# One run for a recurrence head's small products, with the products of its chunk states ahead of it

## The chip, the cores and the metric

The kernel runs on one core of a Trainium2 chip. A core has a matrix engine (TensorE, "PE" in the profile), a vector engine (VectorE, DVE), a scalar engine (ScalarE, ACT), GpSimd (POOL), and SyncE (SP), which here issues DMA transfers. The engines run side by side, each through its own list of instructions in a fixed order, and wait for one another by semaphores. TensorE reads its operands from the on-chip memory SBUF and writes into PSUM banks, which DVE and ACT read.

The metric is the device time of one execution in microseconds. The median of three runs before the change is 448.33 us (448.19 to 448.48).

## What is computed

One layer of a decoder: a projection of 512 tokens into many column groups, a block-sparse attention branch (8 heads of 64), a gated linear recurrence (4 heads, key and value dimension 128), two gated up-projections, an output projection and a gated embedding. The change concerns the recurrence alone. Cut to that:

```python
def hgrn2_chunkwise(q, k, v, g):          # g: logarithm of the decay, per key channel
    def step(state, inp):
        qc, kc, vc, gc = inp
        cum = jnp.cumsum(gc, axis=2)
        o_inter = jnp.einsum('bhtk,bhkv->bhtv', qc * jnp.exp(cum), state)
        diff = jnp.where(causal[:, :, None], cum[:, :, :, None, :] - cum[:, :, None, :, :], LOG_DECAY_MASK)
        scores = jnp.einsum('bhtk,bhsk,bhtsk->bhts', qc, kc, jnp.exp(diff))
        o_intra = jnp.einsum('bhts,bhsv->bhtv', scores, vc)
        last = cum[:, :, -1:, :]
        state = state * jnp.exp(last[:, :, 0, :, None]) + jnp.einsum('bhsk,bhsv->bhkv', kc * jnp.exp(last - cum), vc)
        return state, o_inter + o_intra
```

Each head thus needs the scores inside a chunk (with a decay for every pair of tokens), the state that a chunk hands on, and an output made of both. The output is normalised and gated, and goes into an up-projection.

## The kernel before

**Tiling.** The 512 tokens form four chunks of 128. Large products are split in a high and a low part (three products of 128x128 weights by 512 columns for one, 24 to a block of eight slices, L296 to L302 and L426 to L431). Weights arrive by DMA, ACT and DVE split them (`w_split`, L274), two blocks ahead.

**The recurrence head.** `hgrn_gates` (L513) makes `kb` (keys), `q` (queries, with 16 further columns of 48 for neighbours) and `cum` (the running sum of log decays). `hgrn_intra` (L537) makes the scores inside a chunk from several levels, each with its decays taken against a point between query and key: `k64` and `k32` (`kq`, L544) for far tokens, `next_to` for neighbours, `k8` and `k2` (`fours`, L573) for distances in blocks of 8 and 2. Their products are small. Into the PSUM bank `lpb` go 8 of 64 columns (L639), 8 of 32 (L644) and 16 of 48 (L600, `diag`, "own"); into the bank `lpa` go 16 of 48 for `k8` and 16 for `k2` (L600 too). TensorE makes two passes for each such product, so the profile has two records for one.

These come into the score tile `sc` in several ways: ACT copies the far blocks out (L652, L655); DVE multiplies "own" by a unit mask into `s32` (L648), lays the neighbours over it (`pred_one`, L608) and then six masked copies of the two `lpa` levels (`pred`, L617); last, four ACT copies bring `s32` onto the diagonal of `sc` (L697). All steps on `s32` follow one another on the same tile.

**The chunk state.** `turned_keys` (L660) makes decayed keys, and turns them: a transpose in blocks on DVE (L668), one DMA to DRAM (L671) and four back (L673), from SP's queue, and an ACT copy into `kd` (`turned`, L688). `hgrn_out` (L700) multiplies them with the values of three chunks (`hds`, L706, three full 128x128 products, six records) and chains the three states into `st` (L710, L713), with the decays of whole chunks read out of `cum`, whose exponential stands in `cum` itself (L686). The product `hop` (L721, L723) then takes `sc`, the values, `st` and the decayed queries (L687).

**What sets the order.** TensorE's order is the program's own order. The program counts planned time in `now`: `tick` adds the time of a piece of dense work (0.681 us for three dense products) and lets side work that is due run (`run_due`, L118), `cost` adds without that. Side work is written as generators; what they yield is either planned microseconds or a condition. HP is 2.5 us, HOP 10. `beside_attention` (L508) holds a generator until attention has emitted its next step:

```python
    def beside_attention():
        seen, until = runs[0], now[0] + BESIDE
        if seen < 1000:
            yield lambda: runs[0] > seen or now[0] >= until
```

Attention (L831) has eight steps, two for each head pair, planned 19.5 and 21 us apart; a step emits its scores (L858) and, at every first step from the second pair on, the output with the values (`o`, L906). The hop products of heads 0 to 2 wait in `hops` until a head pair's second step or the next head takes them; those of head 3 come HOP behind its states. Before the first `ub` products the program drains all four recurrence heads (`drain`, L169).

DVE, ACT, POOL and SP are put in order by the compiler's planner, by readiness and program order, with `tc.high_priority` for some. `held` (L156) makes an instruction follow the newest dense product in the planner's order; no semaphore stands for it.

In this order a head has two runs of small products: 48 behind the first `beside_attention` (L639, L644, and two groups of L600), and 16 behind the second (L694 and what follows), directly before `hds`.

**Buffers.** A tag names buffers that tiles share in turn: two for `Q` (the far keys, `k8`, `k2`), eight for `YB` (`ho`, the split results of the heads, later `mh`), two PSUM banks for `g` (`lpb`, `lpa`, `hds`), two for `KT` (`kd` and the turned keys), one for `st` and one for `s32`.

Of the kernel before, what the change touches and what calls it, by code (L numbers as in the profile page):

```python
# [11 lines left out]
F32 = mybir.dt.float32  # L12
# [22 lines left out]
H0 = 8.0  # L35

HOP = 10.0

BESIDE = 30.0

# [30 lines left out]
def hybrid_layer_kernel(  # L71
# [24 lines left out]
    scratch = ctx.enter_context(tc.tile_pool(name="scratch", bufs=2, space=bass.MemoryType.DRAM))  # L96


    BUFS = {"w": 2, "wh": 3, "wl": 3, "A": 16, "X": 16, "YB": 8, "H": 12, "T": 3, "Q": 2, "HQ": 2, "KT": 2, "SG": 4, "VV": 4, "s32": 1, "st": 1, "N": 1, "ps": 8}

    def unit(tag, name, dt=F32, shape=(128, 512)):
        return sb.tile(list(shape), dt, tag=tag, bufs=BUFS[tag], name=name)

# [36 lines left out]
    def cost(us):  # L140
        now[0] += us

    def in_order(inst):

        tc.stamp_issue_order_token(inst.ins, "side")


    dense = []

# [384 lines left out]
        V.tensor_tensor(q[:, :, 0:32], by_block(a), by_block(Q), op=OP.mult)  # L534
        hg[h] = (kb, q, cum)

    def hgrn_intra(h):  # L537
        kb, q, cum = hg[h]
        far = unit("Q", f"hx{h}", shape=(128, 1280))

        def by_block(t):
            return t.rearrange("p (k r) -> p k r", k=16)

        def kq(b, x):  # L544

            n = S // (2 * b)

            def v(t, half):
                return t.rearrange("p (n two b) -> p n two b", two=2, b=b)[:, :, half, :]
            ref = v(cum, 0)[:, :, b - 1:b].to_broadcast([128, n, b])  # L550
            in_order(V.tensor_tensor(v(x, 0), ref, v(cum, 0), op=OP.subtract))
            V.tensor_tensor(v(x, 1), v(cum, 1), ref, op=OP.subtract)
            A.activation(x, x, AF.Exp)
            V.tensor_tensor(v(x, 0), v(kb, 0), v(x, 0), op=OP.mult)
            late = q[:, :, 0:32].rearrange("p (n two g) r -> p n two g r", two=2, g=b // 32)[:, :, 1]
            x1 = v(x, 1).rearrange("p n (g r) -> p n g r", g=b // 32)
            V.tensor_tensor(x1, late, x1, op=OP.mult)
            return x
# [14 lines left out]
        def fours(b):  # L573

            x = unit("Q", f"hx{h}_{b}", shape=(128, 1280))
            keys, turned = x[:, :S], x[:, S:].rearrange("p (n r) -> p n r", r=6 * b)
            n, m = S // (4 * b), S // b

            def blocks(t):
                return t.rearrange("p (m b) -> p m b", b=b)  # L580
            ends = blocks(cum)[:, :, b - 1:b]
            in_order(V.tensor_tensor(blocks(keys), ends.to_broadcast([128, m, b]), blocks(cum), op=OP.subtract))
            late = cum.rearrange("p (n f b) -> p n f b", f=4, b=b)
            lateq = q[:, :, 0:32].rearrange("p k (n r) -> p k n r", r=4 * b)
            for w, o in runs_of(b):
                V.tensor_tensor(turned[:, :, o:o + w * b].rearrange("p n (w b) -> p n w b", w=w), late[:, :, 4 - w:, :],
                                late[:, :, 0:w, b - 1:b].to_broadcast([128, n, w, b]), op=OP.subtract)
            A.activation(x, x, AF.Exp)
            V.tensor_tensor(keys, kb, keys, op=OP.mult)
            for w, o in runs_of(b):  # L590
                t_ = turned[:, :, o:o + w * b].rearrange("p (k n) r -> p k n r", k=16)
                V.tensor_tensor(t_, lateq[:, :, :, (4 - w) * b:], t_, op=OP.mult)
            return x
# [23 lines left out]
                V.copy_predicated(late(s32), late(m), src.rearrange("p c (n r) -> p c n r", r=6 * b)[:, :, :, o:o + w * b])  # L617


        k64 = kq(64, far[:, 0:S])  # L620
        yield HP
        k32 = kq(32, far[:, S:2 * S])
        yield HP
        next_to()
        yield HP
# [2 lines left out]
        yield from beside_attention()  # L628
        while hops:
            hops.pop()()  # L630
        lpb = bank("g", f"lpb{h}")
        big = lpb[:, 256:512].rearrange("p (c t) -> p c t", c=NT)
        own = lpb[:, 0:192].rearrange("p (c t) -> p c t", c=NT)
        lpa = bank("g", f"lpa{h}")[:, 0:384].rearrange("p (l c t) -> p l c t", l=2, c=NT)

        for c in range(NT):
            for half in range(2):
                o, i = c * 128 + 32 * half, 64 * (c % 2) + 32 * half
                PE.matmul(big[i:i + 32, c // 2, :], k64[:, o:o + 32], k64[:, c * 128 + 64:c * 128 + 128],  # L639
                          start=True, stop=True)  # L640
        for c in range(NT):
            for half in range(2):
                o, i = c * 128 + 64 * half, 64 * (c % 2) + 32 * half
                PE.matmul(big[i:i + 32, 2 + c // 2, 0:32], k32[:, o:o + 32], k32[:, o + 32:o + 64], start=True, stop=True)  # L644
        cost(0.3)
        diag(own, kb, q)
        diag(lpa[:, 0], k8[:, :S], by_block(k8[:, S:]))
        V.tensor_tensor(s32, own[:, :, 0:32], eye[:, None, :].to_broadcast([128, NT, 32]), op=OP.mult)  # L648
        scv = sc.rearrange("p (i two) t -> p i two t", two=2)
        for par in range(2):  # L650
            i = 64 * par
            A.activation(scv[0:64, :, par, 64:128], big[i:i + 64, 0:2, :], AF.Copy)  # L652
            for half in range(2):
                j = 64 * half
                A.activation(scv[j:j + 32, :, par, j + 32:j + 64], big[i + 32 * half:i + 32 * half + 32, 2:4, 0:32], AF.Copy)  # L655
        pred_one(own[:, :, 32:48])
        yield HP
        nk = 3 * 128

# [18 lines left out]
            kd, kts = turned_keys()  # L678
            yield HP
        k2 = fours(2)  # L680
        yield 3 * HP
        if not h:
            kd, kts = turned_keys()
        yield 4.0 if h else 8.0

        A.activation(cum, cum, AF.Exp)  # L686
        V.tensor_tensor(q[:, 4:, 0:32], q[:, 4:, 0:32], cum[:, 128:].rearrange("p (k r) -> p k r", r=32), op=OP.mult)  # L687
        turned = A.activation(kd[:, :nk].rearrange("p (c g k) -> p g c k", c=3, g=4),  # L688
                              kts[:, :nk].rearrange("p (g c k) -> p g c k", g=4, c=3), AF.Copy)
        held(turned) if h == 0 else held_from(2.0, [turned], f"hds{h}")  # L690
        yield from beside_attention()
        diag(lpa[:, 1], k2[:, :S], by_block(k2[:, S:]))
        for i in range(2):
            pred(i, lpa[:, i])  # L694
        for g in range(4):
            s_ = slice(32 * g, 32 * g + 32)
            A.activation(sc[s_, :, s_], s32[s_], AF.Copy)  # L697
        hg[h] += (kd,)

    def hgrn_out(h, vb, sbg):  # L700
        kb, q, cum, kd = hg[h][:4]
        hv = slice(h * 128, h * 128 + 128)
        dsp = bank("g", f"hds{h}")
        done.add(f"hds{h}")
        for c in range(3):
            PE.matmul(dsp[:, c * 128:c * 128 + 128], kd[:, c * 128:c * 128 + 128], vb[c][:, hv],  # L706
                      start=True, stop=True)
        cost(0.65)
        st = unit("st", f"st{h}", shape=(128, 3, 128))
        V.tensor_copy(st[:, 0], dsp[:, 0:128])  # L710
        for c in (1, 2):
            e = c * 128 + 127
            V.scalar_tensor_tensor(st[:, c], st[:, c - 1], cum[:, e:e + 1], dsp[:, c * 128:c * 128 + 128],  # L713
                                   op0=OP.mult, op1=OP.add)
        op_ = []

        def products():
            op_.append(bank("a", f"hop{h}"))
            for c in range(NT):
                s_ = slice(c * 128, c * 128 + 128)  # L720
                PE.matmul(op_[0][:, s_], vb[c][:, hv], sc[:, c, :], start=True, stop=(c == 0))  # L721
                if c:
                    PE.matmul(op_[0][:, s_], st[:, c - 1], q[:, 4 * c:4 * c + 4, 0:32], start=False, stop=True)  # L723
            cost(1.5)

        if h < GH - 1:
            hops.append(products)
            yield lambda: op_
        else:
            yield HOP  # L730
            products()
        op_ = op_[0]
        o = unit("YB", f"ho{h}")
        y = unit("N", f"hy{h}")
        A.activation(o, op_, AF.Square)
        gated = f"bg{h}" in done
        if gated:
            V.scalar_tensor_tensor(sbg[h], op_, ogain[:, h:h + 1], sbg[h], op0=OP.mult, op1=OP.mult)
        token_spread(y, token_factor(token_sums(o, y, 1.0 / 128)))
        if gated:  # L740
            V.tensor_tensor(sbg[h], sbg[h], y, op=OP.mult)
        else:
            V.scalar_tensor_tensor(o, op_, ogain[:, h:h + 1], y, op0=OP.mult, op1=OP.mult)
        hg[h] += (None if gated else o,)
# [16 lines left out]
    def recurrence(vb, sbg, res):  # L761
        for h in range(GH):
            yield lambda: h in hg
            if h == 0:
                yield H0
            yield from hgrn_intra(h)
            spawn(hgrn_rest(h, vb, sbg, res))
            yield HP

# [625 lines left out]
```

## Time and profile before

| What | Value |
|---|---|
| median of three runs | 448.33 us (448.19 to 448.48) |
| the profiled execution, its own time | 448.74 us |
| its span on the core | 447.0 us |
| ACT busy | 289.2 us (65%) |
| POOL busy | 89.3 us (20%) |
| instructions | 7843 |

The profile shows one execution. Times inside it count from the start of the span. A row of the chain in order of time has the start, the duration and the line with the number of instructions; a row of a timeline adds the tiles, their sizes and, in brackets, the idle time ahead of it and what ended it. Groups give the busy time and the mean in ns. A matmul's end is modelled, so TensorE is better read by the starts of successive products than by its busy share. The span leaves out 448.74 - 447.0 = 1.7 us around it.

### The profile page before, as it was taken

How to read it: one execution, taken by the hardware profiler on the slowest of the kernel's cores; microseconds unless marked ns; L12 is line 12 of the kernel's file. 1: busy time of each engine (PE TensorE's matmuls, PEld its weight loads, DVE VectorE, ACT ScalarE, POOL GpSimd, SP SyncE). 2: the span in 40 equal slices, each digit the busy share in tenths (PEclk: the TensorE clock that was granted, in tenths of full speed). 3: DMA queues.
4: the chain of work that ended last, by engine and by line, in shares of the span. 5: the costliest groups of instructions: out<-in, count | busy, mean ns of one | idle time of the engine just before them, and what ended most of it. 6: DMA issues, size and time to landing. Idle time of an engine off the chain costs nothing.

```text
span 447.0 us, 7843 instructions
## 1 busy us (share of the span) xinstructions
PE 442.9 (99%) x2808; PEld 374.0 (84%) x2808; DVE 338.7 (76%) x678; ACT 289.2 (65%) x549; POOL 89.3 (20%) x155
## 2 busy tenths in 40 slices
PE   9999999999999999999999999999999999999997
PEld 8888888888888888888888888878888888899996
DVE  5769496786989797958989475565479869998844
ACT  5858484646689888967988697865235434555421
POOL 1000100010000323040402141411210103425520
PEclk9999999999999999999999999999999999999999
DMA  8802333168594464273423643356641544312111
GB/s 253 336 1 95 117 119 114 52 206 189 168 233 130 137 174 134 75 197 119 128 71 109 201 130 132 87 166 167 209 154 46 170 145 154 119 48 94 49 48 47
DMA packets 31958, 59.51 MB, mean 133 GB/s; under 512 B 7088, under 2 KB 16944, under 8 KB 31920
## 3 DMA queue, kind: packets, MB, share of 16 engines
q0 software_dynamic: 10848, 34.87, 24.7%
q1 hardware_dynamic: 20928, 24.14, 19.0%
q8 instruction: 22, 0.36, 0.4%
q14 instruction: 16, 0.13, 0.1%
q10 hardware_dynamic: 144, 0.01, 0.0%
HBM read 48.78 MB, written 4.98 MB: 120 GB/s over the span
## 4 chain that ended last, share of the span: by engine, by line
PE 99%; DVE 0%; issue 0%; DVEq 0%
PE gb L300 10%; PE ga L300 10%; PE h L300 10%; PE g L1260 9%; PE bq L300 5%; PE ub L300 5%; PE aq L430 5%; PE ag L300 5%; PE ak L430 5%; PE bf L300 5%; PE bg L300 5%; PE av L430 5%; PE ua L300 5%; PE bi L430 5%; PE pe L300 2%; PE o L906 2%
## 5 line engine op out<-in xcount | busy, mean ns | idle before, releaser
L282 DVE TENSOR_TENSOR wl<-wf,wh 128x1024 fp32r<-128x1024 f32 (+1 forms) x70 | 77.9, 1112 | 34.5 <-ACT wh L281 34.1
L281 ACT ACTIVATE wh<-wf 128x1024 fp32r<-128x1024 f32 (+1 forms) x70 | 67.0, 958 | 47.6 <-PE ub L300 10.3
L271 POOL DMA_DIRECT2D wf<-in_w_tr_dram x30 | 16.1, 538 | 113.0 <-DVE wl L282 78.1
L893 POOL DMA_DIRECT2D pb<-pb x56 | 27.6, 501 | 38.9 <-DVE pb L882 17.0
L300 PE MATMUL ga<-xh,wh 128*128 128x512 f32 x64 | 25.2, 394 | 0.0
L300 PE MATMUL gb<-xh,wh 128*128 128x512 f32 x64 | 25.1, 393 | 0.0
L300 PE MATMUL ga<-xh,wl 128*128 128x512 f32 x64 | 24.9, 389 | 0.0
L300 PE MATMUL gb<-xl,wh 128*128 128x512 f32 x64 | 24.9, 389 | 0.0
L300 PE MATMUL ga<-xl,wh 128*128 128x512 f32 x64 | 24.9, 389 | 0.0
L300 PE MATMUL h<-mh,wh 128*128 128x512 f32 x64 | 24.9, 389 | 0.0
L300 PE MATMUL h<-ml,wh 128*128 128x512 f32 x64 | 24.9, 389 | 0.0
L300 PE MATMUL h<-mh,wl 128*128 128x512 f32 x64 | 24.9, 389 | 0.0
L300 PE MATMUL gb<-xh,wl 128*128 128x512 f32 x64 | 24.9, 389 | 0.0
L877 ACT ACTIVATE pb<-pb,ps 128x128 f32<-128x128 f32 (+3 forms) x32 | 17.6, 551 | 7.6 <-DVE ps L875 7.0
L271 POOL DMA_DIRECT2D wf<-in_w_tok_dram x8 | 4.4, 550 | 80.8 <-DVE wl L282 77.7
L1236 ACT ACTIVATE sg<-sg 128x256 f32<-128x256 f32 x12 | 5.0, 414 | 20.3 <-DVE sg L1233 20.3
L271 POOL DMA_DIRECT2D wf<-in_w_up_dram x16 | 8.6, 539 | 40.6 <-DVE wl L282 28.1
L879 ACT ACTIVATE pb<-pb,ps 128x128 f32<-128x128 f32 (+3 forms) x32 | 15.8, 550 | 0.1
L300 PEld LDWEIGHTS ga<-xh,wh 128*128 128x128 f32 x64 | 12.0, 188 | 2.8 <-issue 0.4
L300 PEld LDWEIGHTS gb<-xh,wh 128*128 128x128 f32 x64 | 12.0, 188 | 2.8 <-issue 0.2
L300 PEld LDWEIGHTS gb<-xh,wl 128*128 128x128 f32 x64 | 12.0, 188 | 2.5
L300 PEld LDWEIGHTS ga<-xh,wl 128*128 128x128 f32 x64 | 12.0, 188 | 2.5
(956 smaller groups left out, 1449.1 us busy)
## 6 DMA issues: line engine op xcount, KB each, us to landing
wf<-in_w_tr_dram POOLq DMA_DIRECT2D x30, 512.0 KB, 3.8
wf<-in_w_tok_dram POOLq DMA_DIRECT2D x8, 512.0 KB, 3.5
wf<-in_w_up_dram POOLq DMA_DIRECT2D x16, 256.0 KB, 3.0
wf<-in_w_o_dram POOLq DMA_DIRECT2D x8, 512.0 KB, 4.4
wf<-in_w_g_dram POOLq DMA_DIRECT2D x8, 512.0 KB, 3.7
wf<-in_w_tok_dram SPq DMA_DIRECT2D x6, 512.0 KB, 6.9
bias<-in_ed_dram SPq DMA_DIRECT2D x8, 256.0 KB, 4.9
xres<-in_xT_dram SPq DMA_DIRECT2D x8, 256.0 KB, 2.7
```

Of the source, the lines that this page charges most:

```text
L271: (G if len(wraw) >= FAR else nc.sync).dma_start(raw, ap)
L281: rounds[i] = A.activation(hi, wraw[i], AF.Copy)
L282: low = V.tensor_tensor(lo, wraw[i], hi.bitcast(F32), op=OP.subtract)
L300: dense.append(PE.matmul(ps, a[:, k, :], b[k], start=(n == 0), stop=(n == tot - 1)))
L430: dense.append(PE.matmul(banks[t], a[:, s_], b[:, kk, :], start=(k == 0 and i == 0), stop=(k == KD - 1 and i == 2)))
L877: A.activation(p_, p_, AF.Exp, bias=st[:, 0:1], scale=-1.0, accum_out=st[:, 1:2])
L879: A.activation(p_, p_, AF.Copy, scale=st[:, 2:3])
L893: (G if both and b % 2 else nc.sync).dma_start(pt[32 * b:32 * b + 32, a], z[32 * a:32 * a + 32, b])
L906: PE.matmul(o[64 * j:64 * j + 64, qs], va[kb][:, h0:h0 + 64], pt[:, :, 4 * b_ + o0 // 128 + kb, :], start=(kb == 0), stop=(kb == qb))
L1236: A.activation(t[:, c], ps, AF.Sigmoid)
L1260: dense.append(PE.matmul(dst[i], a[:, k], b, start=(m == 0 and i in (1, 6, 5)), stop=(m == 11), skip_group_check=i not in (1, 6, 5)))
```

## The change

The three `hds` products and the chain of states move out of `hgrn_out` into `hgrn_states`, which `hgrn_intra` calls 3 planned us (STATES) behind the ACT copy of the turned keys. That copy is now due 2.5 us behind `k2`'s code for heads 1 to 3, where it was 11.5, and 4 us behind the turned keys for head 0, where it was 8. The decays of whole chunks get a tile of their own, `decay` (128x3). The 48 products move behind the second `beside_attention`, in front of the 16 of `k2`, so that all 64 come in one run; the copies out of their banks move with them, and for the last head they have a higher priority in the planner. hq's scaling moves behind them. `k64` and `k32` become two `YB` tiles instead of one `Q` tile, and `YB` gets a ninth buffer. Head 0's first instruction of `k2` is held behind the newest dense product.

```diff
+STATES = 3.0
...
-    BUFS = {... "YB": 8, ...}
+    BUFS = {... "YB": 9, ...}
...
-        k64 = kq(64, far[:, 0:S])
+        k64 = kq(64, unit("YB", f"hx{h}_64"))
         yield HP
-        k32 = kq(32, far[:, S:2 * S])
+        k32 = kq(32, unit("YB", f"hx{h}_32"))
...
         yield from beside_attention()
         while hops:
             hops.pop()()
-        lpb = bank("g", f"lpb{h}")
...
-        diag(own, kb, q)
-        diag(lpa[:, 0], k8[:, :S], by_block(k8[:, S:]))
...
-        pred_one(own[:, :, 32:48])
         yield HP
...
         k2 = fours(2)
-        yield 3 * HP
+        yield HP if h else 3 * HP
         if not h:
             kd, kts = turned_keys()
-        yield 4.0 if h else 8.0
-
-        A.activation(cum, cum, AF.Exp)
-        V.tensor_tensor(q[:, 4:, 0:32], q[:, 4:, 0:32], cum[:, 128:].rearrange("p (k r) -> p k r", r=32), op=OP.mult)
+            yield 4.0
+        decay = sb.tile([128, 3], F32, tag="decay", bufs=2, name=f"hd{h}")
+        A.activation(decay, cum.rearrange("p (c t) -> p c t", c=NT)[:, 0:3, 127], AF.Exp)
         turned = A.activation(kd[:, :nk].rearrange("p (c g k) -> p g c k", c=3, g=4),
                               kts[:, :nk].rearrange("p (g c k) -> p g c k", g=4, c=3), AF.Copy)
         held(turned) if h == 0 else held_from(2.0, [turned], f"hds{h}")
+        yield STATES
+        st = hgrn_states(h, kd, decay, vb)
+        yield 2 * HP
+        A.activation(cum, cum, AF.Exp)
+        yield HP
         yield from beside_attention()
+        lpb = bank("g", f"lpb{h}")
...
+        diag(own, kb, q)
+        diag(lpa[:, 0], k8[:, :S], by_block(k8[:, S:]))
         diag(lpa[:, 1], k2[:, :S], by_block(k2[:, S:]))
...
+        with tc.high_priority(offset=AHEAD if h == GH - 1 else 0):
+            V.tensor_tensor(s32, own[:, :, 0:32], eye[:, None, :].to_broadcast([128, NT, 32]), op=OP.mult)
...
+            pred_one(own[:, :, 32:48])
+            for i in range(2):
+                pred(i, lpa[:, i])
+            V.tensor_tensor(q[:, 4:, 0:32], q[:, 4:, 0:32], cum[:, 128:].rearrange("p (k r) -> p k r", r=32), op=OP.mult)
+            for g in range(4):
+                s_ = slice(32 * g, 32 * g + 32)
+                A.activation(sc[s_, :, s_], s32[s_], AF.Copy)
+        hg[h] += (st,)
...
+    def hgrn_states(h, kd, decay, vb):
         hv = slice(h * 128, h * 128 + 128)
         dsp = bank("g", f"hds{h}")
         done.add(f"hds{h}")
...
-            V.scalar_tensor_tensor(st[:, c], st[:, c - 1], cum[:, e:e + 1], dsp[:, c * 128:c * 128 + 128],
+            V.scalar_tensor_tensor(st[:, c], st[:, c - 1], decay[:, c:c + 1], dsp[:, c * 128:c * 128 + 128],
                                    op0=OP.mult, op1=OP.add)
+        return st
```

More of the change, by code (lines that the diff above doesn't have):

```diff
@@ L96, in hybrid_layer_kernel @@
     scratch = ctx.enter_context(tc.tile_pool(name="scratch", bufs=2, space=bass.MemoryType.DRAM))
-    BUFS = {"w": 2, "wh": 3, "wl": 3, "A": 16, "X": 16, "YB": 8, "H": 12, "T": 3, "Q": 2, "HQ": 2, "KT": 2, "SG": 4, "VV": 4, "s32": 1, "st": 1, "N": 1, "ps": 8}
+    BUFS = {"w": 2, "wh": 3, "wl": 3, "A": 16, "X": 16, "YB": 9, "H": 12, "T": 3, "Q": 2, "HQ": 2, "KT": 2, "SG": 4, "VV": 4, "s32": 1, "st": 1, "N": 1, "ps": 8}
     def unit(tag, name, dt=F32, shape=(128, 512)):
@@ L145, in in_order @@
         tc.stamp_issue_order_token(inst.ins, "side")
+        return inst
     dense = []
@@ L535, in hgrn_gates, with hgrn_intra @@
         hg[h] = (kb, q, cum)
-    def hgrn_intra(h):
+    def hgrn_intra(h, vb):
         kb, q, cum = hg[h]
-        far = unit("Q", f"hx{h}", shape=(128, 1280))
         def by_block(t):
@@ L581, in fours @@
             ends = blocks(cum)[:, :, b - 1:b]
-            in_order(V.tensor_tensor(blocks(keys), ends.to_broadcast([128, m, b]), blocks(cum), op=OP.subtract))
+            first = in_order(V.tensor_tensor(blocks(keys), ends.to_broadcast([128, m, b]), blocks(cum), op=OP.subtract))
+            if b == 2 and h == 0:
+                held(first)
             late = cum.rearrange("p (n f b) -> p n f b", f=4, b=b)
@@ L630, in hgrn_intra @@
             hops.pop()()
-        lpb = bank("g", f"lpb{h}")
[L632 to L645, printed above, removed]
-        diag(own, kb, q)
-        diag(lpa[:, 0], k8[:, :S], by_block(k8[:, S:]))
[L648 to L655, printed above, removed]
-        pred_one(own[:, :, 32:48])
         yield HP
@@ L690, in hgrn_intra @@
         held(turned) if h == 0 else held_from(2.0, [turned], f"hds{h}")
-        yield from beside_attention()
-        diag(lpa[:, 1], k2[:, :S], by_block(k2[:, S:]))
[L693 to L701, printed above, removed]
+        yield STATES
+        st = hgrn_states(h, kd, decay, vb)
@@ new lines, in hgrn_intra @@
+        yield 2 * HP
+        A.activation(cum, cum, AF.Exp)
+        yield HP
+        yield from beside_attention()
+        lpb = bank("g", f"lpb{h}")
+        big = lpb[:, 256:512].rearrange("p (c t) -> p c t", c=NT)
+        own = lpb[:, 0:192].rearrange("p (c t) -> p c t", c=NT)
+        lpa = bank("g", f"lpa{h}")[:, 0:384].rearrange("p (l c t) -> p l c t", l=2, c=NT)
+        for c in range(NT):
+            for half in range(2):
+                o, i = c * 128 + 32 * half, 64 * (c % 2) + 32 * half
+                PE.matmul(big[i:i + 32, c // 2, :], k64[:, o:o + 32], k64[:, c * 128 + 64:c * 128 + 128],
+                          start=True, stop=True)
@@ new lines, in hgrn_intra @@
+        for c in range(NT):
+            for half in range(2):
+                o, i = c * 128 + 64 * half, 64 * (c % 2) + 32 * half
+                PE.matmul(big[i:i + 32, 2 + c // 2, 0:32], k32[:, o:o + 32], k32[:, o + 32:o + 64], start=True, stop=True)
+        cost(0.3)
+        diag(own, kb, q)
+        diag(lpa[:, 0], k8[:, :S], by_block(k8[:, S:]))
+        diag(lpa[:, 1], k2[:, :S], by_block(k2[:, S:]))
+        with tc.high_priority(offset=AHEAD if h == GH - 1 else 0):
+            V.tensor_tensor(s32, own[:, :, 0:32], eye[:, None, :].to_broadcast([128, NT, 32]), op=OP.mult)
+            scv = sc.rearrange("p (i two) t -> p i two t", two=2)
+            for par in range(2):
+                i = 64 * par
+                A.activation(scv[0:64, :, par, 64:128], big[i:i + 64, 0:2, :], AF.Copy)
+                for half in range(2):
+                    j = 64 * half
+                    A.activation(scv[j:j + 32, :, par, j + 32:j + 64], big[i + 32 * half:i + 32 * half + 32, 2:4, 0:32], AF.Copy)
+            pred_one(own[:, :, 32:48])
[5 more added lines that the diff above has]
+                A.activation(sc[s_, :, s_], s32[s_], AF.Copy)
@@ L711, in hgrn_out @@
         for c in (1, 2):
-            e = c * 128 + 127
-            V.scalar_tensor_tensor(st[:, c], st[:, c - 1], cum[:, e:e + 1], dsp[:, c * 128:c * 128 + 128],
+            V.scalar_tensor_tensor(st[:, c], st[:, c - 1], decay[:, c:c + 1], dsp[:, c * 128:c * 128 + 128],
                                    op0=OP.mult, op1=OP.add)
+        return st
+    def hgrn_out(h, vb, sbg):
+        kb, q, cum, st = hg[h][:4]
+        hv = slice(h * 128, h * 128 + 128)
         op_ = []
@@ L765, in recurrence @@
                 yield H0
-            yield from hgrn_intra(h)
+            yield from hgrn_intra(h, vb)
             spawn(hgrn_rest(h, vb, sbg, res))
```

## The prediction

> **What bounds the kernel.** I read the page's busy times first, then the shares of the chain that ended last, then the waits of PE alone.
>
> ```profile
> span 447.0 us, 7843 instructions
> PE 442.9 (99%) x2808; PEld 374.0 (84%) x2808; DVE 338.7 (76%) x678; ACT 289.2 (65%) x549; POOL 89.3 (20%) x155
> ...
> PE 99%; DVE 0%; issue 0%; DVEq 0%
> ```
> ```profile
> PE warm L195 <- PEq L1383: 0.8, 1, 0.8
> ```
>
> TensorE is busy for 442.9 of 447.0 us, the chain is TensorE's own work, and the one wait of PE in the whole run is 0.8 us before its first product. So nothing that DVE, ACT or a DMA does sets the end today. The change can gain only by making TensorE's own list of products shorter; it loses whatever it makes TensorE wait. No stall is there to be removed.
>
> The list itself is read in the chain in order of time (start, duration, line, count). Head 0 lies inside the aq and ak projections, with no attention near it:
>
> ```profile
> 80.12 0.36 PE lpb L639 x16
> 80.48 0.12 PE lpb L644 x16
> 80.60 0.36 PE lpb L600 x28
> 80.97 0.34 PE lpa L600 x24
> 81.31 2.26 PE aq L430 x9
> ...
> 100.57 0.48 PE lpa L600 x32
> 101.05 0.86 PE hds L706 x6
> 101.92 4.80 PE ak L430 x21
> ```
>
> Head 1 has its first run behind scores and its second behind an attention output:
>
> ```profile
> 154.82 0.36 PE lpb L639 x16
> ...
> 156.01 5.66 PE bq L300 x24
> 161.67 10.88 PE gb L300 x48
> ...
> 180.38 0.48 PE lpa L600 x32
> 180.85 0.86 PE hds L706 x6
> 181.72 1.39 PE bg L300 x6
> ```
>
> And near the end come a hop run and a scores run that go straight back to dense products:
>
> ```profile
> 288.86 0.44 PE hop L721 x4
> ...
> 290.42 6.85 PE ga L300 x30
> 297.27 0.90 PE s L858 x6
> 298.17 3.62 PE ga L300 x15
> ```
>
> The reader is to see four prices. A dense product costs 10.88 / 48 = 0.2267 us. Dense products behind a run of another shape cost more: bq 5.66 - 24 x 0.2267 = 0.22 behind the small products, ga 3.62 - 15 x 0.2267 = 0.22 behind scores, but ga only 6.85 - 30 x 0.2267 = 0.05 behind hop, whose products use the whole array like the dense ones. The second lpa group costs 0.48 where it opens a run, while an equal group that follows another costs 0.34: 0.14 to enter. And hds, six records of a 128-column product, costs 0.86 behind lpa, where hop's records of that size cost 0.44 / 4 = 0.11 each, 0.66 for six: 0.20 for the change of shape.
>
> **The products, part by part.** The change adds and drops none. In the old order a head has a run of 48 (8 + 8 + 16 + 16, two records each), and later a run of 16 followed at once by the three hds. In the new one hds goes alone, some 10 planned us earlier, and all 64 go in one run.
>
> Head 0 before: 81.31 - 80.12 = 1.19 for the first run and 2.26 - 9 x 0.2267 = 0.22 to leave it; 101.92 - 100.57 = 1.35 for the second and 4.80 - 21 x 0.2267 = 0.04 to leave it. Sum 2.80. After: hds between dense products like hop, 0.66 + 0.05; the run of 64, 0.36 + 0.12 + 0.36 + 0.34 + 0.34 = 1.52, and 0.22 to leave it. Sum 2.45, so 0.35 less.
>
> Heads 1 to 3 before, by head 1: 156.01 - 154.82 = 1.19 and 0.22; 181.72 - 180.38 = 1.34 and 1.39 - 6 x 0.2267 = 0.03. Sum 2.78. After, the scores at that place lead back to dense products themselves (0.22), hds costs 0.71, the run of 64 behind the attention output 1.52, and 0.22 to leave. Sum 2.67, so 0.11 less, times three 0.33. All four heads: **about 0.7 us less**. From below, if the longer run and the lone hds keep the full entry prices (0.14 each, eight times 0.14 = 1.1), it would be 0.4 us more; from above, if every dropped border is worth 0.22, see the third rival. I take 0.7, since each term is a row of the same products.
>
> The Trainium skill (TensorE: Matmul & The Clock Gate, section Back-to-back issue gap) gives a product of up to 64 columns a floor of about 25 ns. By it 64 products take 1.6 us in however many runs they come, an estimate, and the gain shrinks by 0.08 a head to 0.4 us. The rows above have 16 products in 0.34 us, 21 ns each, so I keep the rows.
>
> **The order around them.** TensorE's order is the program's, so I added up the due times in the code in steps of 0.681 (three dense products). Head 0's run of 64 now falls behind ak; its planned cost then counts inside the delay before the first scores, which therefore come two dense steps (1.36 us) earlier among the dense products, and the later scores with them by one or two. For heads 1 to 3, hds comes 17 steps behind the first scores of a head pair's second step; the head asks for its place beside attention 29 steps behind, and the next scores come at 31. So the run of 64 stands where the 16 and hds stood, and no head is later.
>
> Does hds wait? Its keys are turned through DRAM, and ACT copies them back before it:
>
> ```profile
> L688 ACT ACTIVATE hkd<-hkt x4: 507/509/512, 95.2 to 270.0; 128x384 f32<-128x384 f32 x4
> ...
> L673 SPq DMA_DIRECT2D hkt<-hkt2there x4: 331/426/490, 188.1 to 189.4; - x4
> ...
> DMA to landing us min/median/max: 1.7/2.0/4.5
> ```
> ```profile
> 273.55 0.65 PE s L858 x7
> ```
>
> Head 2's keys land by 189.4 + 4.5 = 194 us, and its hds, now behind 228.85 (quoted below), moves 15 dense steps and the scores and values of a step ahead, to about 214, so the DMA has 20 us. The copy is tied to a dense product only two steps (1.36 us) ahead of hds and takes 0.51. Today head 3's copy is tied to a product one step before the scores at 273.55, that is at 272.9, yet it ran at 270.0: ACT keeps about 2.9 us ahead of that tie. So I cost this wait at nothing; without that lead it would be 0.51 plus what ACT is in the middle of (under 1.1 us, a weight rounding) less 1.36, up to 0.3 us a head. Behind the copy on ACT stand gate and rounding work that TensorE needs one or two blocks later.
>
> The remaining edits lie off TensorE. The decay tile adds one tiny ACT instruction a head:
>
> ```profile
> 90.35 0.23 ACT L312 ACTIVATE qy<-qt 128x32 f32<-128x32 f32 x1
> ```
>
> At most 0.23 us each by this row, on an engine that is busy 65%: nothing. The states' three DVE instructions move from the crowded stretch behind attention's scores to an emptier one. The keys k64 and k32 in YB buffers, with a ninth, issue the same instructions, live longer, and free the Q buffers sooner; by my count nine YB buffers hold the worst moment (two of head 3, ho of head 2, six finished halves). Head 0's turned keys have the same place; those of the others are issued no later, so SP gets the same transfers. Each is covered by DVE and ACT work that TensorE does not wait for today.
>
> What does lose cover is the tail: the masked copies, the diagonal copies and hq's scaling of the whole head now start only behind the run of 64, and hop needs them all.
>
> ```profile
> 233.28 0.25 DVE L617 COPY_PREDICATED s<-mkf,lpa 128x96 f32<-128x96 int32 x1
> ...
> 243.42 0.31 DVE L617 COPY_PREDICATED s<-mkf,lpa 128x96 f32<-128x96 int32 x1
> ...
> 245.31 0.50 DVE L617 COPY_PREDICATED s<-mkf,lpa 128x64 f32<-128x64 int32 x2
> ...
> 251.51 0.75 DVE L738 SCALAR_TENSOR_TENSOR bg2s<-hop,sm,bg2s 128x512 f32<-128x512 f32 x1 [5.70 <-ACT ho L735]
> ```
> ```profile
> 245.85 1.27 ACT L697 ACTIVATE sc<-s 32x128 f32<-32x128 f32 x4 [1.09 <-DVE s L617]
> ```
> ```profile
> 228.85 0.48 PE lpa L600 x32
> ...
> 249.28 0.44 PE hop L721 x4
> ```
> ```profile
> L687 DVE TENSOR_TENSOR hq<-hq,hu 128x384 f32<-128x384 f32 x4 | 2.2, 540 | 0.0
> ...
> L608 DVE COPY_PREDICATED s<-mkf,lpb 128x64 f32<-128x64 int32 x4 | 1.2, 303 | 0.0
> ...
> L648 DVE TENSOR_TENSOR s<-lpb,mkf 128x128 f32<-128x128 f32 x4 | 1.1, 283 | 0.0
> ```
>
> Head 2's copies end at 245.85 + 1.27 = 247.12, and hop starts at 249.28: 2.16 us of slack. From run to hop it is 27 steps now instead of 28, 1.52 + 0.22 + 27 x 0.681 = 20.1 us instead of 20.4, so 1.9 us of slack remain before anything is added. Added are 0.28 + 0.30 + 0.54 = 1.1 us of DVE work and two more links in the chain, less three state instructions. DVE runs dry behind 245.31 for 5.70 us, so if the late links fall into that gap they cost about 0.3 each, and 1.2 us of slack are left. I cost it at nothing.
>
> **The rivals.** (1) **hop waits for the masked copies** at heads 1 and 2. The first and the fourth copy, with two between, put the links (243.42 - 233.28) / 3 = 3.4 us apart while DVE is full. Two more such links are 6.8 us; the point from which it decides is 1.9 us of added chain. It costs between 0 and 6.8 - 1.9 = 4.9 us at head 2, and less at head 1. For it: the links really are that far apart. Against it: the gap of 5.70 us. With 3 us of wait it gives 448.7 - 0.7 + 3 = 451.0, by the median 450.6: slower. Chance 0.22, small waits elsewhere (a rounding moved by the new DVE order) with it.
>
> (2) **The order is not what I added up**: a head misses its place, which has two steps of margin, and its run comes 27 steps later. Head 3's hop would then follow the scores at 297.27 by more than ten us and the ub products would wait: over 15 us, about 465. Chance 0.02, since the same sum gives every position of the old order.
>
> (3) **Every border between shapes costs its full 0.22.** Head 0 loses two borders (4 to 2), the others one each (7 to 6): five, 1.1 us, 447.2 by the median. For it: both exits into dense products show 0.22. Against it: hds shows 0.20, and the entry 0.14. Chance 0.18. The Trainium skill (TensorEngine Tiling (Array Packing), section Key Properties) says that a change of tiling mode drains TensorE; that is this rival's rule, and the 0.22 behind scores against 0.05 behind hop agrees with it.
>
> **How the numbers follow.** The profiled execution took 448.74, its span 447.0; the median of the runs is 448.33, 0.41 below. 448.74 - 0.7 = 448.0, by the median **447.6**. The forecast itself has 0.58. Its own range, from 0.9 less to 0.4 more, is 447.4 to 448.7; with the third rival below and the milder half of the first above, the range is 447.0 to 450.6. A measurement can tell about 0.2% (0.9 us) from no change: faster, under 447.4, has 0.21 (the third rival and an edge of the forecast); slower, over 449.2, 0.22 (most of the first rival and the second); within 0.57.
>
> **What would show it.** In the chain of the changed kernel hds should stand alone between dense products at about 0.7 us, the run of 64 at about 1.5, and no PE wait beyond the first 0.8. A PE wait at hop on the copies into sc would be the first rival; at hds on ACT's copy, the small price above; scores and run of 64 apart, the second. A smaller hds that is not near 0.7, or dense products behind it with more than 0.05, would break the sum.

## The result, and the profile after the change

The kernel after the change takes **451.73 us** (median of 6 runs, 450.80 to 451.78), the one before 448.36 (6 runs, 448.01 to 448.51): 1.0071 times as long, with a 95% interval of 1.0058 to 1.0084. The forecast was 447.6, its range 447.0 to 450.6. It was wrong in sign and the time lies above the range.

The profiled execution took 451.19 us, with a span of 449.4. First the same three views as before the change: busy times, shares of the chain, waits of PE.

```profile
span 449.4 us, 7830 instructions
...
PE 443.1 (99%) x2808; PEld 372.9 (83%) x2808; DVE 339.0 (75%) x678; ACT 289.0 (64%) x553; POOL 89.2 (20%) x155
...
q8 instruction: 22, 0.36, 0.3%
...
PE 95%; ACT 2%; DVE 1%; issue 1%; DVEq 0%; ACTq 0%
```
```profile
PE lpa L602 <- issue: 1.7, 2, 1.0
...
PE gb L302 <- DVE hk L526: 0.3, 1, 0.3
PE aq L432 <- DVE wl L284: 0.2, 1, 0.2
```

TensorE is as busy as before (443.1 for 442.9), but it now waits. Two waits follow on DVE work; the largest, 1.7 us in two pieces, has "issue" as its cause: nothing that the profile records. The chain in order of time of the kernel after shows where (start, duration, line, count), with head 0, where all is well, for comparison:

```profile
107.19 0.36 PE lpb L680 x16
...
108.04 0.68 PE lpa L602 x48
108.72 2.94 PE bg L302 x12
...
228.03 0.36 PE lpb L680 x16
...
228.88 0.64 PE lpa L602 x45
229.52 0.70 issue
230.22 0.28 PE lpa L602 x5
230.50 0.89 PE bg L302 x3
...
277.36 0.36 PE lpb L680 x16
...
278.72 0.96 issue
279.68 0.38 PE lpa L602 x15
280.05 10.47 PE ga L302 x45
```

At head 0 the run of 64 costs 108.72 - 107.19 = 1.53 and the exit 2.94 - 12 x 0.2267 = 0.22. At head 2 TensorE stops in the middle of the run, and the run costs 230.50 - 228.03 = 2.47; at head 3, 280.05 - 277.36 = 2.69. Against 1.52 that is 0.95 and 1.17, **2.1 us** in all. (The rows of the chain list only some of the small products. The groups of instructions over the same stretches have all 128 records of each run; by them TensorE stops behind the 123rd at head 2 and behind the 112th at head 3.) Head 1, not shown, costs 1.53 like head 0.

The two waits on DVE are read in a timeline, with DVE beside PE (in brackets the idle time and what ended it):

```profile
72.04 0.39 PE L432 MATMUL aq<-wh,xl 128*128 128x512 f32 x1
72.63 0.50 PE L432 MATMUL aq<-wl,xh 128*128 128x512 f32 x1 [0.20 <-DVE wl L284]
72.97 0.39 PE L432 MATMUL aq<-wh,xh 128*128 128x512 f32 x1
...
166.06 0.40 PE L302 MATMUL gb<-xh,wl 128*128 128x512 f32 x1
166.73 0.50 PE L302 MATMUL gb<-xh,wh 128*128 128x512 f32 x1 [0.28 <-DVE hk L526]
167.07 0.40 PE L302 MATMUL gb<-xl,wh 128*128 128x512 f32 x1
```
```profile
64.06 2.10 DVE L588 TENSOR_TENSOR hx<-hu 128x384 f32<-128x384 f32 x6
...
71.39 2.31 DVE L284 TENSOR_TENSOR wl<-wf,wh 128x1024 fp32r<-128x1024 f32 x2
...
166.00 0.68 DVE L526 TENSOR_TENSOR hk<-ha,bf 128x512 f32<-128x512 f32 x1
```

Successive starts say more than the bracket: a dense product follows the last by 0.2267 us, but here by 0.59 and then by 0.34, so the aq wait costs 0.59 + 0.34 - 2 x 0.2267 = 0.48 with its restart, and gb in the same way 0.67 + 0.34 - 0.45 = 0.56. A smaller wait stands ahead of bg at 135.6, where the weight load waits for ACT's softmax (pb, L888): 0.30.

The DVE rows carry the cause of the first. Before the change three subtractions stood at that place:

```profile
64.81 1.10 DVE L586 TENSOR_TENSOR hx<-hu 128x384 f32<-128x384 f32 x3
```

Now there are six, 1.0 us more. k64 and k32 no longer take a `Q` buffer, so `fours(2)` of head 0 finds one free, and only its first instruction is held. The other three subtractions slip in front of hq's product and the weight split, and TensorE waits for both.

So the sum for the kernel after is: 2.12 in the two runs, 0.48 + 0.56 + 0.30 in three waits, less 0.68 of shorter borders (the prediction's sum): 2.8 us. The medians differ by 3.4. In the two chains all heads lie between the first aq and the first ub product, and this stretch takes 301.79 - 60.40 = 241.39 us before the change and 304.13 - 59.65 = 244.48 after it, 3.09 more. (Ahead of aq the profile of before has 0.75 more, in the first products of all, which the change does not touch.)

### The profile page after: what moved, and what is told of

The parts are those of the page before. It is cut to its first block, busy times and chain, and to the rows that moved or that the text cites. A ratio compares the mean times of both kernels' runs of the same rounds, so it can differ in the third digit from the quotient of the medians.

```text
span 449.4 us, 7830 instructions
## 1 busy us (share of the span) xinstructions
PE 443.1 (99%) x2808; PEld 372.9 (83%) x2808; DVE 339.0 (75%) x678; ACT 289.0 (64%) x553; POOL 89.2 (20%) x155
## 4 chain that ended last, share of the span: by engine, by line
PE 95%; ACT 2%; DVE 1%; issue 1%; DVEq 0%; ACTq 0%
PE ga L302 10%; PE h L302 10%; PE g L1271 9%; PE gb L302 9%; PE bg L302 5%; PE ub L302 5%; PE bf L302 5%; PE ak L432 5%; PE ag L302 5%; PE ua L302 5%; PE av L432 5%; PE bi L432 5%; PE aq L432 5%; PE bq L302 4%; PE pe L302 2%; PE o L917 2%
## 5 line engine op out<-in xcount | busy, mean ns | idle before, releaser
L284 DVE TENSOR_TENSOR wl<-wf,wh 128x1024 fp32r<-128x1024 f32 (+1 forms) x70 | 76.5, 1094 | 37.1 <-ACT wh L283 34.5
L888 ACT ACTIVATE pb<-pb,ps 128x128 f32<-128x128 f32 (+3 forms) x32 | 17.6, 551 | 6.9 <-DVE ps L886 6.9
L893 DVE STREAM_TRANSPOSE pb<-pb 128x512 f32<-128x512 f32 x20 | 13.1, 689 | 2.0 <-ACT pb L890 2.0
```

What stands on the lines that cost most here:

```text
L284: low = V.tensor_tensor(lo, wraw[i], hi.bitcast(F32), op=OP.subtract)
L888: A.activation(p_, p_, AF.Exp, bias=st[:, 0:1], scale=-1.0, accum_out=st[:, 1:2])
L893: V.transpose(z[:, :, b_, :].rearrange("p b (n c) -> p b n c", c=32), pb[:, b_].rearrange("p (n b c) -> p b n c", b=4, c=32))
```

## The experiments

**Theory 1** is that the long run outruns the supply of TensorE's instructions. The page has 22 packets of instructions with 0.36 MB: 16.4 KB each. TensorE has 2808 products and 2808 weight loads; 5616 / 22 = 255, so a packet is about 256 instructions, and one small product (two loads and two products) is four of them. A run of 64 is thus one whole block, used up in 1.5 us. **Theory 2**, a rival, is that k2's tile comes late and the record of that wait is missing. **Theory 3** is that the rest of the loss are the waits on DVE and ACT from a new order of their work.

| Run | Kernel | Median us (runs) | Ratio to before, 95% |
|---|---|---|---|
| e1_shift | after, list moved by 160 | 449.88 (10) | 1.0028, 1.0018 to 1.0038 |
| e5_block | after, list moved by 256 | 451.27 (4) | 1.0072, 1.0058 to 1.0086 |
| e11_shift48 | after, list moved by 48 | 451.09 (4) | 1.0059, 1.0047 to 1.0072 |
| e6_before_shift | before, list moved by 160 | 448.16 (10) | 1.0003, 0.9994 to 1.0012 |
| e2_k2first | after, k2's products first in the run | 450.18 (1) | single run, no interval |
| e3_split | after, run cut in 48 and 16 | 451.49 (4) | 1.0070, 1.0052 to 1.0087 |
| e4_due_hold | after, scores 1.38 later, k2 held | 454.55 (4) | 1.0140, 1.0110 to 1.0171 |
| e7_shift_hold | moved by 160, k2 held | 448.87 (11) | 1.0017, 1.0009 to 1.0026 |
| e8_shift_hold_due | moved by 148, held, scores 1.38 later | 450.21 (5) | 1.0045, 1.0032 to 1.0058 |
| e10_shift_hold_step | moved by 160, held, scores 0.7 later | 447.74 (11) | 0.9990, 0.9982 to 0.9999 |
| e9_states | after, run of 48 back at its old place | 451.55 (6) | 1.0075, 1.0060 to 1.0089 |

Before took 448.50 beside e1 to e4, 448.04 beside e5 to e8 and 448.36 beside e9 to e11.

### e1_shift: the same work, another place in the list

```diff
-    for i in range(WARM):
+    for i in range(5):
         PE.matmul(warm[:, 0:128], one, one, start=True, stop=True)
+    for i in range(44):
+        j = 32 * (i % 4)
+        PE.matmul(warm[j:j + 32, 0:32], one[:, 0:32], one[:, 0:32], start=True, stop=True)
```

The first products write a bank that nobody reads; here 4 of them are left out and 44 small ones added, 160 instructions more, all ahead of the first weights.

> The changed kernel, with TensorE's list of instructions moved by 160: of its nine first products (which compute nothing that is used) five stay and 44 small ones of the same kind follow, at about the time of the four left out. Nothing else differs. Theory 1 (TensorE runs out of fetched instructions in the run of 64: 256 instructions in 1.5 us, and the two gaps of 0.70 and 0.96 us in the lpa products of heads 2 and 3 are a block of instructions that has not landed): the block borders fall elsewhere in the run, both gaps go or move to another head, and PE's wait for nothing, 1.7 us, changes by over 0.5 us. Theory 2 (the k2 factors or the bank come late): both gaps stay within 0.2 us.

1.85 us less than the kernel after, for a change that touches no head. In the chain of this kernel head 2's run has no gap:

```profile
229.03 0.36 PE lpb L683 x16
...
229.88 0.68 PE lpa L605 x64
230.56 0.90 PE bg L305 x3
```

### e5_block, e11_shift48, e6_before_shift: the controls

e5 has 68 small products in place of 44 (256 instructions, a whole block); e11 keeps 8 of the first products and adds 13 small ones (48); e6 is e1's edit on the kernel before.

> The kernel after, with TensorE's list moved by 256 instructions (4 of the 9 unused first products left out, 68 small unused ones added): one whole block of instructions. Theory 1 (a run of 64 outruns the supply where a block's border falls at its start): a block's border lies again where it lay in the kernel after, so the two gaps inside lpa at heads 2 and 3 are back, 0.5 to 1.2 us each at the same place near the run's end, and the time is 451.0 to 452.0. Rival (the shift by 160 helped because the start of the kernel is another, or because the added products warm something up): no gaps, 449.9 as with the shift by 160.

> The kernel after with its list moved by 48 instructions only (1 of the 9 unused first products left out, 13 small ones added). From the places of the gaps so far, a block's border stands 10 instructions ahead of head 2's run in the kernel after, 32 ahead of head 3's and 16 inside head 1's, and the next 256 later. Theory 1: moved by 48, the border stands 32 ahead of head 1's run, as it did at head 3, so head 1, which had no gap, gets one of 0.7 to 1.2 us about 48 records into lpa; heads 2 and 3, with borders 58 and 80 ahead, amid the slower o products, have none or under 0.2. Time: the kernel after less 2.1 plus 1.0, 450.2 to 450.9. Rival (gaps belong to the heads, to their data or their place in time): gaps again at heads 2 and 3 and none at head 1, or at none, 449.9.

> The kernel before, with its list moved by 160 as in the first experiment (4 unused first products left out, 44 small ones added). Theory 1: a run of 48 with its 192 instructions never holds a whole block beside dense products, so there is no gap with either place of the borders, and the time is that of before, 448.4 within 0.3. Rival (the shift itself gains, whatever the runs): about 1.8 us less, 446.6.

The chain of e5, heads 2 and 3, and then that of e11, head 1 and head 2:

```profile
229.84 0.64 PE lpa L605 x59
230.48 0.69 issue
...
279.16 0.51 PE lpa L605 x48
279.67 0.67 issue
280.35 0.38 PE lpa L605 x15
```
```profile
181.08 0.49 PE lpa L605 x35
181.58 0.95 issue
182.53 0.40 PE lpa L605 x17
...
230.62 0.68 PE lpa L605 x48
231.30 0.91 PE bg L305 x3
```

Moved by a whole block, both gaps are back at the same products, behind the 123rd and the 112th record. Moved by 48, the gap leaves heads 2 and 3 and appears at head 1, as worked out beforehand from the places of the borders; e11's time is 0.2 us above the expected range. The kernel before does not care for the shift (1.0003; from the first aq to the first ub product its chain takes 241.39 us with the shift, as without). So the gap belongs to the place in the list, not to a head, its data or the warming products.

The transfers fit. In a narrow window of the view of DMA, here 227.8 to 228.0 of the kernel after, one packet of instructions starts, right at the beginning of head 2's run:

```profile
DMA packets 1, 0.02 MB, mean 82 GB/s; under 512 B 0, under 2 KB 0, under 8 KB 0
...
q8 instruction: 1, 0.02, 28.7%
```

The share, 28.7% of 16 engines for 0.2 us, is 0.92 us for this packet. TensorE goes on at 230.22, 2.2 to 2.4 us after the packet's start. The same reading gives 2.5 to 2.7 at head 3 (packet between 277.0 and 277.2, resumed at 279.68), 2.3 to 2.5 and 2.2 to 2.5 in e5, 2.5 to 2.7 in e11, and 2.2 to 2.6 in the five gaps of e2 and e4 (below). A block asked for at a border can be used only some 2.5 us later, and a run of 64 eats the block before it in 1.5. By this reading the gap, about 1 us, comes when a border falls close to the start of a run; with the border further off, the block also holds slower products of o or dense ones. A packet at the start of a run is not enough: at head 1 of the kernel after one starts between 179.4 and 179.6, the run at 179.61, and there is no gap. Its border can be counted from the gaps that head 1 gets when instructions are added ahead of it: behind record 111, 222 instructions in, with 48 added (e11), and behind record 129, 258 in, with 12 (e4, below). Both put it 14 instructions inside the run of the kernel after (222 + 48 - 256 and 258 + 12 - 256), so the block ends only seven dense products, 1.6 us, behind the run. The old runs of 48 and 16 hold 192 and 64 instructions, never a whole block.

The Trainium skill (Runtime: NRT & Kernel Launch, section Instruction fetch mechanics) says that instructions are refilled in blocks of 16 KiB, 256 of them, and that the next is fetched while the present one executes; the 16.4 KB above agree. It also calls the cost of a border "mostly hidden", since dispatch is slower than the fills; by that the run would cost 1.5 everywhere, and the gaps of 0.67 to 0.96 here speak against it for products of 21 ns.

### e2_k2first and e3_split: is k2 late, and what a cut costs

e2 moves k2's 16 products from the end of the run to its front; e3 puts a planned 2.5 us between the 48 and the 16.

```diff
+        yield HP
         diag(lpa[:, 1], k2[:, :S], by_block(k2[:, S:]))
```

> The changed kernel with the 16 products of k2 at the front of the run of 64 instead of its end. Theory 1 (instructions run out): the gap stays where it is counted in instructions, near the end of the run, now in the k8 products, still 0.7 and 1.0 us at heads 2 and 3. Theory 2 (k2 comes late): the gap stands in front of the run or behind its first products, at k2.

> The changed kernel with 2.5 planned us of dense products between the 48 and the 16 products of k2. Theory 1 (instructions run out): neither part has 256 instructions, the gaps of heads 2 and 3 go (2.1 us with what they cost behind them), and each head pays another border, 0.14 + 0.22, 1.4 us in all: 0.5 to 1 us faster than the changed kernel, about 451. If the run's length had nothing to do with it, it would be 1.4 us slower than the changed kernel, about 453.

With k2 first, the gaps stand near the run's end as before, now inside k8's products, which had long been ready, and behind the 123rd and the 112th record again (chain of e2, head 2):

```profile
227.46 0.48 PE lpa L602 x32
...
228.65 0.30 PE lpa L602 x27
228.94 0.56 issue
229.50 0.28 PE lpa L602 x5
```

Theory 2 falls. Cut in two, the run has no gap, yet next to nothing is won: 451.49 is 0.24 below the kernel after, where 0.5 to 1 was expected, and the intervals overlap. Each head pays its border again, and head 3's outputs, later now, make ub wait (waits of PE in e3):

```profile
PE ub L302 <- ACT ybh L233: 0.6, 1, 0.6
```

### e4, e7, e8 and e10: the waits on DVE and ACT

e4 holds all four subtractions of head 0's k2 and moves the first scores by 1.38 planned us; e7 is e1 with the holding alone; e8 and e10 add the scores' move to it, by 1.38 and by 0.7. The edits:

```diff
-                V.tensor_tensor(turned[:, :, o:o + w * b]...
+                then = V.tensor_tensor(turned[:, :, o:o + w * b]...
...
+                if b == 2 and h == 0:
+                    held(then)
...
-        yield 5.0 - BIAS0
+        yield 5.0 - BIAS0 + 0.7
```

> The changed kernel with attention due 1.38 planned us later, so that its steps stand where they stood before among the dense products, and with all four subtractions of head 0's k2 held behind the newest dense product instead of the first alone. Theory 3 (the rest of the loss, about 1.2 us, is TensorE waiting for a split weight in aq, because k2's subtractions stand in front of it on DVE, and for PSUM banks in gb and bg, because scores come two dense steps earlier): these three waits go, 0.9 to 1.3 us faster than the changed kernel, and the gaps in the run of 64 stay or move a little, as the list differs by some 12 instructions at heads 1 to 3. Otherwise: within 0.3 us of the changed kernel.

> The first experiment (list moved by 160) and all four subtractions of head 0's k2 held behind the dense product, where the kernel after holds only the first. Theory 3 (three subtractions of 0.35 us ahead of hq's product and of the weight split on DVE make the aq products wait): the two aq waits (0.9 on hq, 0.2 on the split, about 1.3 to 1.5 lost with their restart) go, and 449.9 falls to 448.3 to 448.7, the time of before. Rival (DVE has slack there, the waits are of one profile only): 449.9 stays.

> As the run before it, and the first scores due 1.38 planned us later, so that they stand among the dense products where they stood before the change; the list is moved by 148, since this order puts 12 more instructions ahead of the runs of heads 1 to 3. Theory 3: the waits of gb on hk (0.3 to 0.6) and of bg on pb (0.2 to 0.4) go too, no gap in the instruction supply is left, and the time is 447.5 to 448.1, below before. Rival (moving the scores brings the wait of o on the masked softmax, 1.3 us with 0.4 of small gaps around it, as it did with the unmoved list): 449.0 to 449.8.

> The list moved by 160, the four subtractions of head 0's k2 held, and the first scores due 0.7 planned us later: each head pair's first scores then come one dense step earlier than before the change (two in the kernel after), its second scores and o where they stood before (one step earlier in the kernel after, one later with 1.38). Theory 3: o does not wait (it did where the scores stood a step too late), the wait of gb on hk (0.56 in the place lost) gets smaller or goes, and the time lies between 447.5 and 448.4, at or below before. Rival (waits come back elsewhere at any place of the scores): 448.9 or more, as without the move.

e4 was a miss. The waits of aq, gb and bg went, but the order put 12 more instructions ahead of the runs of heads 1 to 3. The gaps of heads 2 and 3 moved by just that: they stand behind the 117th and the 106th record, six records and their six weight loads earlier. At head 1 a border now fell just behind the run, and the scores, a dense step too late at head 2, made o wait (waits of PE in e4):

```profile
PE bg L302 <- issue: 1.8, 1, 1.8
PE lpa L604 <- issue: 1.5, 2, 0.8
PE o L919 <- DVE ps L888: 1.3, 1, 1.3
```

These 4.6 us outweigh what was won. In e8, moved by 148 to undo the 12, no gap was left, but the wait of o stayed: 450.21, a little above its rival's range. Of e7 the profile has neither aq wait; against e1 the ratio falls by 0.0011, 0.5 us, where 1.3 to 1.5 was expected, and the two intervals overlap. The 0.9 us wait on hq in e1's profile, taken from the slowest of its ten runs (450.22), is probably too large for the typical one (the kernel after has 0.2, on the weight load alone). What remains in e7 is gb's 0.3 and, on the weight load, the wait of bg on the softmax. In e10 the view of waits of PE has one row only, the wait ahead of its first product that all these kernels have:

```profile
PE warm L197 <- PEq L1399: 0.8, 1, 0.8
```

447.74 us, 0.62 below before, interval 0.9982 to 0.9999. This version has the whole change in it, with the list moved, k2 held and the first scores 0.7 later, and it beats both kernels, narrowly.

### e9_states: half of the change

> Half of the change: the chunk states' products stand ahead as in the kernel after, but the run of 48 is back at its old place, so each head has a run of 48, hds alone and a run of 16; the rest (decay tile, YB buffers for k64 and k32, the one held subtraction) is as after. By the prices read in the chain, head by head: 1.19 + 0.22 and 0.67 + 0.05 and 0.48 + 0.22, 2.83 instead of 2.78 (0.2 in all). Theory 1: no run of 64, so no gap in the supply of instructions; theory 3: the freed Q buffer still puts three subtractions ahead of hq and the split, 0.5 to 1.3, and the scores come one step early, up to 0.5. Together 448.7 to 450.0 with no gap inside lpa. Rival (the gaps come with the early states, not with the long run): gaps again, 450.5 or more.

The run of 48 (L680 to the second group of L602) with its copies goes back behind the first `beside_attention`; only the chunk states stay early. No gap inside lpa, as theory 1 has it, but 451.55, above the range expected, for other waits:

```profile
PE gb L302 <- DVE hk L526: 1.4, 1, 1.4
...
PE hds L713 <- DVE s L610: 0.4, 1, 0.4
```

In the chain of e9 ACT's copies into sc, the copy of the turned keys and the gates of head 2 stand one behind the other from 160.8 to 166.0, and gb waits for the gates behind them; hds waits for a bank that a masked copy still reads. So the early states bring waits of their own where the run of 48 is not moved with them, and theory 3's size for them was too small by 1.5 us at least.

## Why the prediction was wrong, point by point

**The bound** was read rightly: no stall was there to remove, and the change "loses whatever it makes TensorE wait".

**The prices of the borders** held at head 0 and came out a little low at the others. hds stands alone at 0.67, dense products behind it show 4.81 - 21 x 0.2267 = 0.05 (below), the fed run takes 1.53, its exit 0.22. Head 0 is 0.67 + 0.05 + 1.53 + 0.22 = 2.47 against 2.45. Where neither gaps nor waits are left, in e10, the whole is 0.62 less by the medians, against 0.7. That agreement is in part luck: from the first aq to the first ub product e10's chain is only 0.39 shorter than before, 300.35 - 59.35 = 241.00 against 241.39. Head 0 gains its 0.33, but at heads 1 to 3 the dense products behind the run and behind the scores lose some 0.27 each time, not 0.22; in the chain of e10 5.71 - 24 x 0.2267 and 9.11 - 39 x 0.2267 are both 0.27 (second view). The floor of about 25 ns that the Trainium skill (TensorE: Matmul & The Clock Gate, section Back-to-back issue gap) gives for a product of up to 64 columns did not bind: 32 in 0.68 are 21 ns.

```profile
214.04 0.67 PE hds L713 x6
214.71 4.81 PE gb L302 x21
```
```profile
228.53 5.71 PE ag L305 x24
...
249.60 9.11 PE gb L305 x39
```

**The step that failed first** is the sum "the run of 64, 0.36 + 0.12 + 0.36 + 0.34 + 0.34 = 1.52", taken "since each term is a row of the same products". The rows came from runs of 48 and of 16; that a longer run at the same rate can run out of something was not asked. The runs showed 2.47 and 2.69 at heads 2 and 3. The upper bound for that price, "0.4 us more" for all four heads, looked at shapes alone.

**The step that failed second** is the last of the costs at nothing: "Each is covered by DVE and ACT work that TensorE does not wait for today." The prediction had said that the new buffers "free the Q buffers sooner", and that the scores "come two dense steps (1.36 us) earlier", but priced neither. The first lets three subtractions ahead of hq and a weight split (0.48 us at the split, gone when they are held), the second puts scores and softmax ahead of head 2's gates, which hold the bank that gb needs (0.56), and lets bg wait for a softmax (0.30); both are gone in e10, where the scores are one step later.

**The order** was as added up: the first scores two steps earlier, hds and the run of 64 at the places given, no head late. **hds does not wait** in the kernel after; in e8, with the scores' move, it did, by 0.4, where up to 0.3 had been named.

**The rivals.** hop waits nowhere: the tail of masked copies fitted, and the slower case that held 0.22 came true by another mechanism. The order's rival did not occur. "Every border costs its full 0.22" is refuted by the 0.05 behind hds. The range ended at 450.6 since its only dear case was hop.

**What stays open.** Of the 3.09 us between the two chains 2.8 are added up above; most of the rest are the 0.05 more at each exit to dense products at heads 1 to 3. The 0.3 from there to the 3.4 between the medians are not in these two profiles. Why the packet at head 1 of e4 starts so late, between 181.0 and 181.2 with the run at 179.82 (the gap of 1.77 is the longest), was not tried, nor why in e8 and e4 o needs the bank just when it does. e10's three parts were not tried without the shift.

## What to carry to other kernels

A price per product read from a short run is not the price in a longer one: count the instructions, ask whether a whole block of them is used up faster than the next arrives, and, since any edit ahead of the run moves the borders, compare with a shifted control. A freed buffer and an earlier due time change the order on every engine: look for what moves ahead of the instruction that TensorE needs next, and price it, above all where the gain on the critical engine is small.

## What the hardware showed that was not expected

TensorE stopped for 0.56 to 1.77 us with "issue" as the only cause, when a border between blocks of 256 instructions fell close to the start of a run of 64 products of 21 ns: by the counts of these runs with the border 44, 34, 32, 22 or 10 instructions ahead of it or 2 inside, and not with 14 inside or 58 ahead. From the start of a packet to the resumption it took 2.2 to 2.7 us, in ten gaps. Adding unused products ahead of all work, 160 instructions, made the same kernel 1.85 us faster, and 256 made it as slow as before the shift.
